# A list scheduler's planning figures replaced by trace durations, and the MLP's squares taken from Pool to Scalar

## The chip, the core and the metric

One core of a Trainium2 chip runs the whole program in one launch. The time is the device time of one execution in microseconds (us). The kernel before took 1974.14 us, the median of three runs (1968.65 to 1974.84). The engines are TensorE (PE in the profile, with its weight loads as PEld), Vector (DVE), Scalar (ACT), Pool (POOL) and Sync (SP), which only issues DMAs.

## What is computed

Two blocks on 512 tokens of width 1024, in float32. The first has two layers, each with a mixer (chunked mLSTM, a Fourier mix and a gated convolution) and an MLP, on the tokens and, in layer 0, on 256 context tokens too. The second is one layer of sparse, windowed, pooled and memory attention. The MLP is the part whose squares change:

```python
def sq_relu_mlp(h, w1, w2):
    return jnp.square(jax.nn.relu(h @ w1)) @ w2

x = x + mx[5] * rmsnorm(sq_relu_mlp(hx, w_mlp1[l], w_mlp2[l]), g_post_mlp[l])
```

## The kernel before

Activations lie transposed, 128 features by tokens. Each large product is done in three passes of a reduced format: an operand x is split into hi (x rounded) and lo (x - hi), and hi*hi, hi*lo and lo*hi are summed in PSUM. `split` makes such a pair with a Scalar copy and a Vector subtraction; `weight` loads a weight block into a `wr` buffer and splits it into `wh` and `wl`. Tiles named `pd`, `pm` and `pa` are PSUM; `slot`, `tmp`, `ftmp` and `small` are SBUF buffers.

The MLP's hidden width of 4096 is worked in eight quarters of four blocks. A block's first product is evacuated by `first` or, for the pairs done by a Strassen scheme in `strassen`, by `fast`'s `tail`: a relu on Scalar, then `square_parts`, which must leave hi and lo of the square for the second product. In the first quarter (`plain`), Vector and Pool also build the Strassen combinations of the inputs (`combos`). Before the MLP of a layer come its mixer, whose mLSTM runs chunk by chunk (`scores`, `values`, `outputs`, `turned`), and the product with w_out (`Wo`, in `layer`).

Nothing is issued as it is written. Every operation is recorded with its dependencies, and `Recorder.schedule` walks a simulated clock: at each moment it gives every free engine the ready operation of the lowest priority number for which buffers are free. `Recorder.cost` says how many nanoseconds an operation takes in that plan, and constants in `schedule` say how much later a dependent operation may start on the same or another engine. The resulting order is then written out by `issue`, each engine working strictly in its own order and waiting by semaphores. So a figure in `cost` changes no instruction; it changes where instructions stand. All recorded operations carry the line of `issue` (L395), so the profile is read by tile names.

Of the kernel before, what the change touches and what calls it, by code (L numbers as in the profile page):

```python
# [13 lines left out]
F32 = mybir.dt.float32  # L14
# [3 lines left out]
AF = mybir.ActivationFunctionType  # L18
ALU = mybir.AluOpType
# [110 lines left out]


class Op:
    __slots__ = ("eng", "fn", "method", "a", "k", "deps", "out", "n", "prio", "bufs", "start", "end", "cost", "dma")


class Recorder:
# [75 lines left out]
    def cost(self, op, out):  # L212
        if out is None:
            return 1300
        if op.dma:
            x = out if isinstance(out, View) else (op.k["in_"] if "in_" in op.k else op.a[1])
            return math.prod(x.shape) * 4 / 330
        n = max(out.idx.size, max((v.idx.size for v in op.a if isinstance(v, View)), default=0))
        if op.eng == "pe":
            if op.method == "transpose":  # L220
                return 110
            lhs = op.a[1]
            n = out.idx.size
            if lhs.dtype == F32R:
                return n / 2.4 + 2 if n >= 256 else 107
            if lhs.dtype == BF:
                return max(n / 2.4, 61)
            c = max(4 * n / 2.4, 217)
            return c / 4 + 26 if lhs.shape[1] <= 32 else c / 2 if lhs.shape[1] <= 64 else c
        ins = [v for v in list(op.a[1:]) + [op.k.get("in_"), op.k.get("in0")] if isinstance(v, View)]  # L230
        psum = any(v.buf.kind in PSUM_KINDS for v in ins)
        if op.eng == "act":
            ap = sum(isinstance(op.k.get(x), View) for x in ("bias", "scale"))
            return (55 if psum else 97) + 0.833 * n + 93 * ap + (93 if "accum_out" in op.k else 0)
        if op.eng == "vec":
            if op.method == "reciprocal":
                return 70 + 8 * n
            if op.method in ("tensor_copy", "tensor_scalar", "memset") and not psum:
                return 70 + 0.55 * n + (120 if op.method == "tensor_scalar" else 0)
            return (135 if op.method == "scalar_tensor_tensor" else 70) + 1.042 * n  # L240
        if op.method == "tensor_tensor":
            return 150 + 2.1 * n
        if op.method == "tensor_scalar":
            return 200 + 3.6 * n
        return 100 + 0.85 * n

    def schedule(self):

        ops = self.ops
# [22 lines left out]
        free = {k: [(0.0, i) for i in range(n or 0)] for k, (n, _) in self.kinds.items()}  # L272
        engs = {"pe": 0.0, "act": 0.0, "vec": 0.0, "pool": 0.0, "sp": 0.0}
# [5 lines left out]
        def push(i, t):  # L279
            heapq.heappush(waiting[ops[i].eng], (t, i))  # L280
# [2 lines left out]
                push(i, 0.0)  # L283
        done = 0
        now = 0.0
        SEM, SLACK, SAME = 120.0, 300.0, {"pe": 0.0, "act": 120.0, "vec": 130.0, "pool": 60.0, "sp": 0.0}
        releases = []

        def place(o):

            new = [b for b in o.bufs if b.place is None]
            got = []
            for b in new:
                n, spare = self.kinds[b.kind]
# [12 lines left out]
                got.append(b)  # L307
            for b in new:
                b.place = heapq.heappop(free[b.kind])[1] if b in got else next(self.names)
            return True  # L310
        while done < N:
            progress = False
            for e in ("sp", "pe", "vec", "act", "pool"):
                while waiting[e] and waiting[e][0][0] <= now:
                    i = heapq.heappop(waiting[e])[1]
                    heapq.heappush(avail[e], (ops[i].prio, i))
                if engs[e] > now or not avail[e]:
                    continue
                skipped, pick = [], None
                if e == "pe" and held is not None:  # L320
                    x = (ops[held].prio, held)
                    if x not in avail[e] or not place(ops[held]):
                        continue
                    avail[e].remove(x)
                    heapq.heapify(avail[e])
                    pick = held
                while avail[e] and pick is None:
                    x = heapq.heappop(avail[e])
                    if place(ops[x[1]]):
                        pick = x[1]  # L330
# [12 lines left out]
                o.start = now  # L343
                if o.dma:
                    issue = {"sp": 60, "act": 60, "pool": 1040}[e]
                    engs[e] = now + issue
                    dma_free[e] = max(dma_free[e], now + issue) + o.cost
                    o.end = dma_free[e] + 1900
                else:
                    engs[e] = o.end = now + o.cost  # L350
                order.append(pick)
                done += 1
                for b in o.bufs:
                    b.left -= 1
                    b.end = max(b.end, o.end)
                    if b.left == 0 and self.kinds[b.kind][0] is not None:
                        heapq.heappush(free[b.kind], (b.end + SEM, b.place))
                        heapq.heappush(releases, b.end + SEM)
                for j in succ[pick]:
                    same = ops[j].eng == e and not o.dma  # L360
                    wait = SAME[e] if same else SEM + (SLACK if ops[j].eng == "pe" else 0)
                    ready_at[j] = max(ready_at[j], o.end + wait)
                    need[j] -= 1
                    if need[j] == 0:
                        push(j, ready_at[j])
            if progress:
                continue
            ts = [t for t in engs.values() if t > now] + [w[0][0] for w in waiting.values() if w and w[0][0] > now]
            while releases and releases[0] <= now:
                heapq.heappop(releases)  # L370
# [27 lines left out]
def tile_net(tc: tile.TileContext, A, out):  # L398
    rec = Recorder(tc.nc, tc, KINDS)
    act, vec, pool, pe, sp = [rec.engine(e) for e in ("act", "vec", "pool", "pe", "sp")]  # L400

    def kind(k):
        return lambda shape=(P, 512), dt=F32: rec.buf(k, shape, dt)
    slot, tmp, ftmp, small, const, rst, pd, pm, pa = [kind(k) for k in ("slot", "tmp", "ftmp", "small", "const", "rs", "pd", "pm", "pa")]

    def A_(out_, in_, f, bias=0.0, scale=1.0):
        return act.activation(out_, in_, f, bias=bias, scale=scale)
# [24 lines left out]
    for l in range(2):  # L432
        t = const([P, NPV], F32)
# [957 lines left out]
    def layer(l, hs, nxt, steps, back, mid, ends, early=None, norm_mem=None, fill=None):  # L1391
# [52 lines left out]

        def second(q, b, g, o):
            w, sl, n = g
# [695 lines left out]
```

## Time and profile before

| | |
|---|---|
| median of 3 runs | 1974.14 us |
| profiled execution | 1975.36 us, span 1973.6 us |
| TensorE matmul busy | 1890.9 us (96%) |
| Vector busy | 1354.0 us (69%) |
| Scalar busy | 908.9 us (46%) |
| Pool busy | 425.8 us (22%) |
| mean granted TensorE clock | 0.980 |

The span runs from the first to the last instruction. A matmul's end is modelled, and matmuls overlap, so the start of one to the start of the next is what it costs in a row. The granted clock is a share of full speed, 2.4 GHz; 0.50 is the lower level, 1.2 GHz. "idle before" names the engine and tile that ended a wait.

### The profile page before, as it was taken

How to read it: one execution, taken by the hardware profiler on the slowest of the kernel's cores; microseconds unless marked ns; L12 is line 12 of the kernel's file. 1: busy time of each engine (PE TensorE's matmuls, PEld its weight loads, DVE VectorE, ACT ScalarE, POOL GpSimd, SP SyncE). 2: the span in 40 equal slices, each digit the busy share in tenths (PEclk: the TensorE clock that was granted, in tenths of full speed). 3: DMA queues.
4: the chain of work that ended last, by engine and by line, in shares of the span. 5: the costliest groups of instructions: out<-in, count | busy, mean ns of one | idle time of the engine just before them, and what ended most of it. 6: DMA issues, size and time to landing. Idle time of an engine off the chain costs nothing.

```text
span 1973.6 us, 32415 instructions
## 1 busy us (share of the span) xinstructions
PE 1890.9 (96%) x12772; PEld 1641.0 (83%) x12772; DVE 1354.0 (69%) x2370; ACT 908.9 (46%) x1786; POOL 425.8 (22%) x438
## 2 busy tenths in 40 slices
PE   5999998998999999999989999889999999999999
PEld 3978886787888999999978888778989889888777
DVE  6499768368356556665677968577787778657686
ACT  4532256564323322332573345655334347556554
POOL 1110042215112211221301023233232221111321
PEclk8999999898999999999999999899999999999999
DMA  8233235243233112211361123352323244311121
GB/s 312 90 110 108 96 109 177 68 150 107 96 118 126 65 56 75 76 65 54 108 216 68 54 86 140 107 171 81 112 86 116 98 137 162 109 54 44 46 84 65
DMA packets 82714, 207.47 MB, mean 105 GB/s; under 512 B 8961, under 2 KB 36865, under 8 KB 82562
## 3 DMA queue, kind: packets, MB, share of 16 engines
q1 hardware_dynamic: 66114, 188.86, 28.0%
q10 hardware_dynamic: 16448, 16.54, 2.5%
q8 instruction: 100, 1.64, 0.3%
q14 instruction: 52, 0.43, 0.1%
HBM read 189.12 MB, written 16.25 MB: 104 GB/s over the span
## 4 chain that ended last, share of the span: by engine, by line
PE 80%; DVE 11%; ACT 3%; DMA 2%; issue 2%; POOL 1%; SPq 0%; DVEq 0%; POOLq 0%; ACTq 0%
PE pd L395 57%; PE pm L395 21%; DVE slot L395 7%; PE pa L395 3%; DVE tmp L395 2%; ACT slot L395 1%; DVE wl L395 1%; DMA wr<-in_w_ada 1%; DVE small L395 1%; ACT tmp L395 1%; DMA wr<-in_w_in 1%; ACT small L395 1%; DMA slot<-in_w_ada 1%; ACT wh L395 0%; DVE ftmp L395 0%
## 5 line engine op out<-in xcount | busy, mean ns | idle before, releaser
L395 PE MATMUL pd<-slot,wh 128*128 128x256 f32 (+2 forms) x4384 | 1092.2, 340 | 14.5 <-DVE slot L395 5.5
L395 PEld LDWEIGHTS pd<-slot,wh 128*128 128x128 f32 (+1 forms) x4384 | 744.7, 189 | 122.0 <-issue 17.5
L395 PE MATMUL pd<-slot,wl 128*128 128x256 f32 (+1 forms) x2136 | 720.9, 339 | 4.9 <-DVE wl L395 4.7
L395 PEld LDWEIGHTS pd<-slot,wl 128*128 128x128 f32 x2136 | 406.8, 191 | 52.1 <-DVE wl L395 6.8
L395 ACT ACTIVATE wh<-wr 128x1024 fp32r<-128x1024 f32 (+2 forms) x202 | 204.9, 1015 | 387.4 <-PE pd L395 356.3
L395 DVE TENSOR_TENSOR wl<-wr,wh 128x1024 fp32r<-128x1024 f32 (+2 forms) x199 | 244.7, 1230 | 128.5 <-ACT wh L395 126.3
L395 PE MATMUL pm<-slot,slot 128*128 128x256 f32 (+3 forms) x1674 | 238.0, 291 | 6.9 <-ACT slot L395 4.0
L395 PEld LDWEIGHTS pm<-slot,slot 128*128 128x128 f32 x1674 | 213.2, 191 | 19.7 <-issue 6.4
L395 DVE TENSOR_TENSOR slot<-pd,slot 128x512 f32<-128x512 f32 (+1 forms) x208 | 119.5, 574 | 122.3 <-PE pd L395 120.4
L395 PE MATMUL pd<-slot,slot 128*128 128x256 f32 (+1 forms) x1048 | 143.0, 285 | 2.4 <-ACT ftmp L395 1.6
L395 PEld LDWEIGHTS pd<-slot,slot 128*128 128x128 f32 x1048 | 130.1, 189 | 8.4 <-issue 3.5
L395 ACT ACTIVATE tmp<-tmp 128x512 f32<-128x512 f32 (+3 forms) x122 | 62.2, 545 | 123.1 <-DVE tmp L395 122.1
L395 DVE TENSOR_TENSOR slot<-ftmp,slot 128x512 fp32r<-128x512 f32 (+2 forms) x116 | 90.9, 786 | 36.5 <-POOL ftmp L395 35.0
L395 DVE SCALAR_TENSOR_TENSOR slot<-slot,const,slot 128x512 f32<-128x512 f32 (+2 forms) x184 | 113.5, 664 | 0.8
L395 POOL TENSOR_TENSOR ftmp<-tmp 128x512 f32<-128x512 f32 x54 | 58.8, 1110 | 214.1 <-ACT tmp L395 214.0
L395 POOL TENSOR_TENSOR ftmp<-ftmp 128x256 f32<-128x256 f32 (+1 forms) x72 | 62.4, 867 | 186.5 <-ACT ftmp L395 154.8
L395 POOL TENSOR_TENSOR wr<-wr 128x512 f32<-128x512 f32 x27 | 39.3, 1456 | 286.4 <-DVE wl L395 247.2
L395 DVE TENSOR_TENSOR slot<-wr,slot 128x512 fp32r<-128x512 f32 (+1 forms) x85 | 86.0, 1018 | 20.8 <-ACT slot L395 20.8
L395 PE MATMUL pm<-slot,wh 128*128 128x256 f32 x544 | 98.4, 281 | 0.0
L395 ACT ACTIVATE slot<-wr 128x512 fp32r<-128x512 f32 (+1 forms) x85 | 72.1, 854 | 44.1 <-POOL wr L395 22.6
L395 ACT ACTIVATE slot<-tmp 128x512 fp32r<-128x512 f32 (+1 forms) x122 | 73.5, 627 | 31.5 <-DVE tmp L395 18.8
L395 PEld LDWEIGHTS pm<-slot,wh 128*128 128x128 f32 x544 | 84.2, 188 | 2.8 <-issue 1.6
(202 smaller groups left out, 2355.3 us busy)
## 6 DMA issues: line engine op xcount, KB each, us to landing
wr<-in_w_mlp SPq DMA_DIRECT2D x128, 512.0 KB, 3.4
wr<-in_w_ada SPq DMA_DIRECT2D x80, 512.0 KB, 3.8
wr<-in_w_in SPq DMA_DIRECT2D x66, 512.0 KB, 3.3
dram<-slot ACTq DMA_DIRECT2D x52, 256.0 KB, 3.3
tmp<-dram SPq DMA_DIRECT2D x40, 256.0 KB, 3.6
slot<-in_w_ada SPq DMA_DIRECT2D x16, 512.0 KB, 9.3
wr<-in_w_out SPq DMA_DIRECT2D x16, 512.0 KB, 4.1
wr<-in_w_out SPq DMA_DIRECT2D x8, 384.0 KB, 2.9
```

The lines of the kernel that those rows point to most:

```text
L395: o.fn(*[conv(x) for x in o.a], **{k: conv(x) for k, x in o.k.items()})
```

## The change

There are two edits. The planner's figures are rewritten: `cost` gets new formulas by engine and shape, and `schedule` gets new waits between engines, a charge of 170 ns where TensorE goes from one array shape to another, and a longer Vector operation where it and a Pool operation both read two tiles from SBUF. And `square_parts` no longer lets Pool multiply the tile with itself: Scalar squares in place, and `split` copies the result to hi on Scalar and subtracts on Vector.

```diff
             lhs = op.a[1]
+            op.mode = tuple(32 if x <= 32 else 64 if x <= 64 else 128 for x in (k, lhs.idx.size if op.method == "transpose" else lhs.shape[1]))
             if lhs.dtype == F32R:
-                return n / 2.4 + 2 if n >= 256 else 107
+                return n * 0.4453 + 4 if n >= 256 else 112
...
         if op.eng == "act":
-            return (55 if psum else 97) + 0.833 * n + 93 * ap + (93 if "accum_out" in op.k else 0)
+            return (150 + 0.86 * n if psum else 190 + 0.847 * n) + 97 * ap + (195 if op.k.get("accum_out") is not None else 0)
         if op.eng == "vec":
...
-            return (135 if op.method == "scalar_tensor_tensor" else 70) + 1.042 * n
+            return (200 if op.method == "scalar_tensor_tensor" else 140) + 1.06 * n
         if op.method == "tensor_tensor":
-            return 150 + 2.1 * n
+            return 200 + 2.1 * n
...
-        SEM, SLACK, SAME = 120.0, 300.0, {"pe": 0.0, "act": 120.0, "vec": 130.0, "pool": 60.0, "sp": 0.0}
+        SAME = {"pe": 0.0, "act": 35.0, "vec": 35.0, "pool": 70.0, "sp": 0.0}
+        SEM, TO = {"pe": 205.0}, {"pe": 420.0, "pool": 80.0}
+        SWITCH, mode = 170.0, None
+        reads = {"vec": 0.0, "pool": 0.0}
...
+                    if e == "pe":
+                        if mode != o.mode:
+                            engs[e] = o.end = o.end + SWITCH
+                        mode = o.mode
+                    elif e in reads and o.shared:
+                        if e == "vec" and reads["pool"] > now:
+                            engs[e] = o.end = o.end + 0.6 * min(reads["pool"] - now, o.cost)
+                        reads[e] = o.end
...
-                    wait = SAME[e] if same else SEM + (SLACK if ops[j].eng == "pe" else 0)
+                    wait = SAME[e] if same else max(SEM.get(e, 40.0), TO.get(ops[j].eng, 0.0))
...
         def square_parts(t, ah, al):
-            A_(ah, t, AF.Square)
-            t2 = ftmp(list(t.shape))
-            pool.tensor_tensor(t2, t, t, op=ALU.mult)
-            vec.tensor_tensor(al, t2, ah.bitcast(F32), op=ALU.subtract)
+            A_(t, t, AF.Square)
+            split(ah, al, t)
```

Where the instructions stand is seen in the order that each engine is given. Scalar, in the first quarter of layer 0's MLP, before: each tile (`ftmp`, from `pd`) has a relu and a square into a `slot`; between them stand the modulations (`tmp` with two `const`) of the context tokens.

```order
L395 ACTIVATE ftmp_676_4449<-pd_620_4129 128x256
L395 ACTIVATE tmp_671_4417<-tmp_671_4417,const_57_258,const_469_3118 128x256
L395 ACTIVATE slot_680_4465<-ftmp_676_4449 128x256
L395 ACTIVATE slot_608_4044<-tmp_671_4417 128x512
L395 ACTIVATE ftmp_682_4479<-pd_622_4136 128x256
```

The same place after the change:

```order
L411 ACTIVATE ftmp_675_4447<-pd_621_4127 128x256
L411 ACTIVATE ftmp_677_4454<-pd_627_4169 128x256
L411 ACTIVATE ftmp_675_4447<-ftmp_675_4447 128x256
L411 ACTIVATE ftmp_677_4454<-ftmp_677_4454 128x256
L411 ACTIVATE slot_681_4473<-ftmp_675_4447 128x256
L411 ACTIVATE slot_682_4480<-ftmp_677_4454 128x256
```

Two tiles now go through relu, square and copy side by side, and the second half of the modulation has moved behind them.

Vector, at the end of that quarter, before. A row `slot<-ftmp,slot` of 256 columns is a square's subtraction, the last one here being that of the ninth tile; rows with `tmp` and 512 columns are the Strassen combinations and their splits; `wl` is a weight's lower half.

```order
L395 TENSOR_TENSOR slot_688_4520<-ftmp_706_4661,slot_688_4520 128x256
L395 TENSOR_TENSOR wl_710_4683<-wr_665_4387,wh_709_4668 128x1024
L395 TENSOR_TENSOR slot_610_4054<-tmp_693_4551,slot_608_4044 128x512
L395 TENSOR_TENSOR slot_694_4556<-ftmp_712_4692,slot_694_4556 128x256
L395 TENSOR_TENSOR slot_711_4687<-tmp_705_4650,slot_711_4687 128x512
L395 TENSOR_TENSOR slot_719_4730<-tmp_701_4614,slot_711_4687 128x512
L395 TENSOR_TENSOR wl_721_4741<-wr_668_4403,wh_717_4717 128x1024
L395 TENSOR_TENSOR slot_680_4465<-ftmp_718_4726,slot_680_4465 128x256
```

After the change, with the ninth tile's subtraction in the fourth row:

```order
L411 TENSOR_TENSOR slot_606_4035<-tmp_679_4463,slot_605_4028 128x512
L411 TENSOR_TENSOR slot_699_4652<-tmp_689_4531,slot_699_4652 128x512
L411 TENSOR_TENSOR wl_703_4687<-wr_664_4382,wh_700_4660 128x1024
L411 TENSOR_TENSOR slot_681_4473<-ftmp_701_4674,slot_681_4473 128x256
L411 TENSOR_TENSOR slot_707_4718<-tmp_680_4465,slot_699_4652 128x512
L411 TENSOR_TENSOR wl_709_4727<-wr_667_4402,wh_705_4708 128x1024
L411 TENSOR_TENSOR slot_682_4480<-ftmp_704_4694,slot_682_4480 128x256
L411 TENSOR_TENSOR slot_707_4718<-tmp_692_4571,slot_707_4718 128x512
L411 TENSOR_TENSOR tmp_712_4759<-slot_619_4123,tmp_695_4610 128x512
```

A weight half, combinations and splits that stood ahead of the ninth tile's subtraction now stand behind it.

TensorE, at the end of the mLSTM of layer 1, before: `pm` with 129 columns are values, the last ones in the first row; `pd` with 512 columns is w_out's product; `pm<-const` are transposes. The rows between the first and the last are all there is between the two.

```order
L395 MATMUL pm_1765_12182<-slot_1652_11663,slot_1611_11443 128x129 x2
L395 MATMUL pd_1753_12134<-slot_1699_11870,wh_1746_12110 128x512 x2
L395 MATMUL pd_1753_12134<-slot_1699_11870,wl_1751_12126 128x512
L395 MATMUL pd_1767_12195<-slot_1694_11852,wh_1760_12156 128x512 x2
L395 MATMUL pd_1767_12195<-slot_1694_11852,wl_1762_12169 128x512
L395 MATMUL pd_1767_12195<-slot_1694_11852,wh_1760_12156 128x512
L395 MATMUL pd_1767_12195<-slot_1697_11863,wh_1760_12156 128x512
L395 MATMUL pd_1767_12195<-slot_1694_11852,wl_1762_12169 128x512
L395 MATMUL pd_1767_12195<-slot_1697_11863,wh_1760_12156 128x512 x2
L395 MATMUL pd_1767_12195<-slot_1697_11863,wl_1762_12169 128x512
L395 MATMUL pd_1767_12195<-slot_1699_11870,wh_1760_12156 128x512 x2
L395 MATMUL pd_1767_12195<-slot_1699_11870,wl_1762_12169 128x512
```

After the change:

```order
L411 MATMUL pm_1698_12129<-slot_1588_11636,slot_1534_11304 128x129
L411 MATMUL pm_1699_12136<-slot_1478_10820,slot_1679_12016 128x129 x2
L411 MATMUL pm_1701_12143<-slot_1588_11636,slot_1543_11375 128x129 x2
L411 MATMUL pd_1687_12072<-slot_1641_11839,wh_1632_11803 128x512
L411 MATMUL pd_1687_12072<-slot_1641_11839,wl_1635_11818 128x512
L411 MATMUL pm_1702_12160<-const_33_130,slot_1657_11907 128x128
L411 MATMUL pm_1703_12162<-const_33_130,ftmp_1629_11796 128x128 x2
```

Fifteen of w_out's matmuls stood behind the last values; two do now, and the others stand ahead of them.

## Rows read from the trace of the kernel before

**Rows 1.** The page, part 1: busy us, share of the span and instructions by engine.

```profile
PE 1890.9 (96%) x12772; PEld 1641.0 (83%) x12772; DVE 1354.0 (69%) x2370; ACT 908.9 (46%) x1786; POOL 425.8 (22%) x438
```

**Rows 2.** Span and mean granted clock of the core.

```profile
core 0: 1973.6 us, clock 0.980
```

**Rows 3.** Windows: length, PE, PEld, DVE, ACT, POOL busy (count), clock, DMA share, GB/s.

```profile
450.00:500.00 50.00, 45.59 (x305) 39.08 (x305) 38.63 (x46) 24.58 (x53) 27.17 (x22) 0.90 0.21 74
700.00:750.00 50.00, 50.00 (x345) 46.32 (x344) 28.48 (x40) 13.91 (x21) 9.59 (x8) 1.00 0.13 43
1300.00:1350.00 50.00, 42.34 (x298) 37.18 (x299) 40.91 (x48) 26.38 (x55) 27.09 (x22) 0.97 0.33 119
```

**Rows 4.** Windows, same columns: two stretches of low clock, and one ahead.

```profile
487.60:494.40 6.80, 6.08 (x18) 4.85 (x19) 2.96 (x10) 2.47 (x6) 1.57 (x2) 0.50 0.23 78
1225.00:1235.00 10.00, 8.19 (x48) 6.70 (x47) 10.00 (x39) 7.83 (x26) 0.00 (x0) 1.00 0.34 125
1235.10:1245.40 10.30, 5.79 (x14) 3.14 (x15) 4.29 (x9) 8.17 (x24) 2.24 (x2) 0.50 0.00 0
```

**Rows 5.** In order of time, steady MLP: start, us, engine, line, operation, out<-in.

```profile
697.28 1.14 ACT L395 ACTIVATE slot<-tmp 128x512 fp32r<-128x512 f32 x2
...
699.85 0.68 DVE L395 TENSOR_TENSOR slot<-ftmp,slot 128x512 fp32r<-128x512 f32 x1
```

**Rows 6.** Groups by form, 450 to 500: count, busy us, mean ns, idle before.

```profile
L395 POOL TENSOR_TENSOR ftmp<-ftmp 128x256 f32<-128x256 f32 x12 | 11.7, 973 | 8.5 <-ACT ftmp L395 8.3
...
L395 DVE TENSOR_TENSOR slot<-tmp,slot 128x512 fp32r<-128x512 f32 x12 | 13.0, 1093 | 0.0
L395 DVE TENSOR_TENSOR slot<-ftmp,slot 128x256 fp32r<-128x256 f32 x12 | 9.1, 759 | 0.5 <-ACT ftmp L395 0.5
...
L395 ACT ACTIVATE slot<-ftmp 128x256 fp32r<-128x256 f32 x12 | 4.9, 412 | 0.2
```

**Rows 7.** Groups by form, 1300 to 1350.

```profile
L395 POOL TENSOR_TENSOR ftmp<-ftmp 128x256 f32<-128x256 f32 x12 | 11.0, 920 | 26.4 <-issue 21.5 <-DVE slot L395 2.4 <-PE pm L395 1.8
...
L395 DVE TENSOR_TENSOR slot<-tmp,slot 128x512 fp32r<-128x512 f32 x12 | 10.5, 898 | 0.0
L395 DVE TENSOR_TENSOR slot<-ftmp,slot 128x256 fp32r<-128x256 f32 x12 | 10.1, 844 | 1.3 <-POOL ftmp L395 1.3
```

**Rows 8.** TensorE's waits, 450 to 500: us in total, times, longest.

```profile
PE pd L395 <- DVE slot L395: 2.6, 2, 2.2
PE pd L395 <- ACT ftmp L395: 1.6, 1, 1.6
```

**Rows 9.** TensorE's longest waits, 1300 to 1350.

```profile
PE pd L395 <- DVE wl L395: 4.2, 2, 3.4
```

**Rows 10.** In order of time, 480 to 490, Vector and Pool.

```profile
483.15 1.75 POOL L395 TENSOR_TENSOR tmp<-tmp,slot 128x512 f32<-128x512 f32 x1
...
483.66 1.52 DVE L395 TENSOR_TENSOR slot<-ftmp,slot 128x256 fp32r<-128x256 f32 x1
485.10 1.28 DVE L395 TENSOR_TENSOR slot<-tmp,slot 128x512 fp32r<-128x512 f32 x2
...
487.86 0.41 DVE L395 TENSOR_TENSOR slot<-ftmp,slot 128x256 fp32r<-128x256 f32 x1
```

**Rows 11.** In order of time, TensorE at five places, with idle time before.

```profile
145.58 0.66 PE L395 MATMUL pm<-const,slot 128*128 128x128 f32 x4 [2.81 <-DVE slot L395]
...
425.45 0.80 PE L395 MATMUL pm<-tmp,const 128*128 128x256 f32 x1 [4.42 <-DVE tmp L395]
...
475.93 3.11 PE L395 MATMUL pd<-slot,slot 128*128 128x256 f32 x24 [1.63 <-ACT ftmp L395]
...
1223.70 0.48 PE L395 MATMUL pd<-slot,wh 128*128 128x512 f32 x1
...
1236.12 0.86 PE L395 MATMUL pm<-const,slot 128*128 128x128 f32 x2 [2.93 <-ACT slot L395]
```

**Rows 12.** In order of time, Scalar, the split of w_out's weight.

```profile
1222.02 1.04 ACT L395 ACTIVATE wh<-wr 128x1024 fp32r<-128x1024 f32 x1
```

More of the change, by code (lines that the diff above doesn't have):

```diff
@@ L132 @@
 class Op:
-    __slots__ = ("eng", "fn", "method", "a", "k", "deps", "out", "n", "prio", "bufs", "start", "end", "cost", "dma")
+    __slots__ = ("eng", "fn", "method", "a", "k", "deps", "out", "n", "prio", "bufs", "start", "end", "cost", "dma", "mode", "shared")
 class Recorder:
@@ L219, in cost @@
         if op.eng == "pe":
+            lhs = op.a[1]
+            k = lhs.p1 - lhs.p0
+            op.mode = tuple(32 if x <= 32 else 64 if x <= 64 else 128 for x in (k, lhs.idx.size if op.method == "transpose" else lhs.shape[1]))
             if op.method == "transpose":
                 return 110
-            lhs = op.a[1]
             n = out.idx.size
             if lhs.dtype == F32R:
-                return n / 2.4 + 2 if n >= 256 else 107
+                return n * 0.4453 + 4 if n >= 256 else 112
@@ L226, in cost @@
             if lhs.dtype == BF:
-                return max(n / 2.4, 61)
-            c = max(4 * n / 2.4, 217)
-            return c / 4 + 26 if lhs.shape[1] <= 32 else c / 2 if lhs.shape[1] <= 64 else c
+                return max(n / 2.4 + 2.5, 61)
+            c = max(4 * n / 2.4 + 5, 219)
+            return c / 4 + 2 if op.mode == (128, 32) else c / 2 if op.mode == (128, 64) else c
         ins = [v for v in list(op.a[1:]) + [op.k.get("in_"), op.k.get("in0")] if isinstance(v, View)]
         psum = any(v.buf.kind in PSUM_KINDS for v in ins)
+        op.shared = len(ins) > 1 and not psum
@@ L232, in cost @@
         if op.eng == "act":
-            ap = sum(isinstance(op.k.get(x), View) for x in ("bias", "scale"))
-            return (55 if psum else 97) + 0.833 * n + 93 * ap + (93 if "accum_out" in op.k else 0)
+            ap = any(isinstance(op.k.get(x), View) for x in ("bias", "scale"))
+            return (150 + 0.86 * n if psum else 190 + 0.847 * n) + 97 * ap + (195 if op.k.get("accum_out") is not None else 0)
         if op.eng == "vec":
             if op.method == "reciprocal":
-                return 70 + 8 * n
+                return 137 + 8 * n
@@ L238, in cost @@
             if op.method in ("tensor_copy", "tensor_scalar", "memset") and not psum:
-                return 70 + 0.55 * n + (120 if op.method == "tensor_scalar" else 0)
-            return (135 if op.method == "scalar_tensor_tensor" else 70) + 1.042 * n
+                return (200 if op.method == "tensor_scalar" else 150) + 0.65 * n
+            return (200 if op.method == "scalar_tensor_tensor" else 140) + 1.06 * n
         if op.method == "tensor_tensor":
-            return 150 + 2.1 * n
+            return 200 + 2.1 * n
@@ L243, in cost @@
         if op.method == "tensor_scalar":
-            return 200 + 3.6 * n
-        return 100 + 0.85 * n
+            return 350 + 2.8 * n
+        return 110 + 0.85 * n
     def schedule(self):
@@ L356, in schedule @@
                     if b.left == 0 and self.kinds[b.kind][0] is not None:
-                        heapq.heappush(free[b.kind], (b.end + SEM, b.place))
-                        heapq.heappush(releases, b.end + SEM)
+                        heapq.heappush(free[b.kind], (b.end + 120.0, b.place))
+                        heapq.heappush(releases, b.end + 120.0)
                 for j in succ[pick]:
                     same = ops[j].eng == e and not o.dma
-                    wait = SAME[e] if same else SEM + (SLACK if ops[j].eng == "pe" else 0)
+                    wait = SAME[e] if same else max(SEM.get(e, 40.0), TO.get(ops[j].eng, 0.0))
                     ready_at[j] = max(ready_at[j], o.end + wait)
```

## The prediction

> **What bounds the kernel now.** I read the page first, then the clock, then windows of 50 us, then what TensorE waits for in the windows that are not full, then single stretches instruction by instruction. TensorE is busy 1890.9 us of 1973.6 [rows 1], and the change touches no matmul. So the time can move only where TensorE is not fed: 82.7 us without a matmul, and the stretches in which its clock is at the lower of its two levels (the mean granted clock is 0.980 [rows 2], which is some 40 us at full speed). The windows show where. From 700 to 750 us, in the middle of an MLP, TensorE is busy 50.00 of 50.00 at clock 1.00, and nothing that another engine saves there counts. From 450 to 500 and from 1300 to 1350, at the start of the two MLPs, it is busy 45.59 and 42.34, the clock is 0.90 and 0.97, and Vector and Pool are at their busiest [rows 3]. The kernel is a full engine with some forty small holes; a new order closes some and opens others.
> A wait costs more than its length. With the one that ends at 488.3 the granted clock falls to 0.50 (1.2 GHz) for 6.80 us, with the one before 1236.12 for 10.30 us [rows 4]. A matmul takes twice as long there, so up to 3.4 and 5.1 us go on top.
>
> **The squares.** 106 tiles (54 of 512 columns, 52 of 256) lose Pool's product and gain a Scalar copy. Vector's subtraction stays and reads the squared tile instead of Pool's.
> Most of this is hidden. In the steady MLP of layer 0 the last two tiles of a Strassen product show the tightest case: Scalar squares both from 697.28 in 1.14 us, Vector ends the last subtraction at 700.53 [rows 5]. Without Pool, Scalar copies both right behind, until about 699.5 (another pair, 1.05 to 1.14 us), and the last subtraction (0.68) ends at about 700.2. Equal or 0.3 us earlier, and TensorE does not idle there. Price 0; bounds per round: nothing gained, since the engine is full, or 0.5 us lost; over seven rounds 0 to +3.5 us. Scalar's extra work, 54 x 0.6 + 52 x 0.41 = 54 us [rows 5, 6], lies where Scalar is busy 14 to 26 of 50 us [rows 3].
>
> It isn't hidden in the first quarter of either MLP, where Vector is the bound: TensorE waits 2.6 us for Vector's slot tiles and 1.6 us for a square's Scalar chain in the first stretch, 4.2 us for Vector's weight halves in the second [rows 8, 9]. Pool slows Vector there. The subtraction of 256 columns takes 0.41 us at 487.86, with Pool idle, and 1.52 us at 483.66, while Pool is in a tensor_tensor from 483.15 to 484.90 [rows 10]. Over the first stretch its mean is 0.759 us, and that of the 512 column splits 1.093 [rows 6] against 0.68 alone [rows 5]: 12 x 0.35 + 12 x 0.41 = 9.1 us of Vector's time that Pool costs. Pool's squares are 11.7 of its 27.2 us there [rows 3, 6], 43%, so 3.9 us go with them. In the second stretch the same sum is 12 x 0.434 + 12 x 0.218 = 7.8 us, the squares are 11.0 of 27.1 us [rows 3, 7], and 3.2 us go. Scalar, which takes over, gets 12 x 0.41 = 4.9 us in each stretch, beside 25 and 26 us.
> The new order helps in the first stretch as well. The subtraction for which TensorE waits until 488.3 stood behind most of the Strassen combinations on Vector; several of them now stand behind it, some 6 us of Vector's work.
> I take away 2.4 us of waits for Vector in the first stretch (all but 0.2 of them) and 3.1 in the second, together 5.5, and 3.1 of the low clock that comes with them (3.4 us in the first; in the second a mean of 0.97 over 50 us, 1.5). Bounds: nothing, if Scalar's longer chain takes Vector's place; and all of it, 4.2 + 4.2 + 4.9 = 13.3 us. **Term: -8.6 us.**
>
> **The planner's numbers.** They shift instructions everywhere, yet on TensorE the neighbourhood of most waits stays: the same matmuls stand around the waiting one, moved by a few microseconds. I price a shift with 0.12 us for a matmul of 256 columns (24 of them in the 2.94 us from 475.93 [rows 11]) and 0.23 for one of 512. Three waits get more cover: the one of 2.81 us before 145.58, the one of 4.42 before 425.45 [rows 11], and the first one's repeat in layer 1, before 1092.3. TensorE's work ahead of them grows by 1.0, 2.6 and 0.9 us, Vector's by -0.5, 1.2 and 0.0: together 3.8 us gained. In the start-up eleven matmuls fewer stand ahead of a wait near 51, up to 1.3 us lost, and 0.5 at the one before it; I take half, 0.9. At the end of the mLSTM of layer 1, fifteen matmuls of w_out (512 columns) stood between the last values and the transposes that wait; now two do. 13 x 0.23 = 3.0 us of cover is gone, and the wait of 2.93 us before 1236.12 [rows 11] can become 5.9. It need not: Vector is busy 10.00 of 10.00 us from 1225 to 1235 [rows 4], and where it is behind anyway, values that come later cost nothing. Bounds 0 and 3.0, I take 1.5. Sum of what I can place: -3.8 + 0.9 + 1.5 = -1.4. New waits can't be seen in the old trace, and a new order makes some; I set them at +1.4, so this term is **0**. Its bounds: -16.5 (the three waits wholly gone, 10.1 us, and with each a low clock of at most the 3.4 us priced above, less the 3.8 counted), and +7, rival C.
> I credit the plan with no more because its new figures are not the time for which an engine is held. A 512 column tensor_tensor is now planned as 140 + 1.06 x 512 = 683 ns, which is what one shows, but two in a row from 485.10 take 1.28 us [rows 10]: the second starts after 0.60, and 603 ns is what the old formula gave.
> The Trainium skill (Perfetto Trace Analysis, Optimizing Scalar/DVE Operations) speaks against the change in the same way: a profiled duration contains a tail that overlaps the next instruction. By that rule the planner's term is 0 or worse; taking durations as occupancy it would be -3.8.
> Loads: as many DMAs are issued, and SP's list has as many rows; I leave them at 0, bounds within those of this term.
>
> **Sum.** The profiled execution took 1975.36 us (the span of 1973.6 and 1.8 around it), 1.2 over the median of 1974.14. 1975.4 - 8.6 + 0 = 1966.8; counted from the median, 1965.5. I say 1966.
>
> **Rivals.**
> A. The order pays as well: the three waits with more cover go (6.3 us beyond the 3.8), and half of the low clock with them (5.1). 1966 - 11.4 = 1955. For it: the cover grows at all three. Against: only 3.8 of the 10.1 us are in the order.
> B. The squares give nothing: TensorE waits for relu, square and copy on Scalar where it waited for Vector, or for the combinations that were moved back. 1974. For it: one wait in the first stretch (1.63 us before 475.93 [rows 11]) already names Scalar. Against: Scalar has half its time free there.
> C. Slower, at the end of the mLSTM of layer 1. The w_out matmuls are spent early: 3.0 us. They also stand 2.9 us earlier in TensorE's work, while their split weight was ready at 1223.06 for a use at 1223.70 [rows 11, 12], so up to 2.3 us of a new wait. A longer hole can lengthen the 10.30 us of low clock there [rows 4]; by a third, that is 1.7 lost. 7.0 us; with the squares giving nothing, 1982. It decides from the point where Vector is no longer behind TensorE at 1225, and wins over the forecast where the squares give less than 7.
>
> **Chances.** The forecast (the squares pay, the plan is even) 0.45, its own range 1958 to 1973; A 0.15; B 0.20; C 0.20. A measurement of this kernel can tell 0.3%, 5.9 us, from no change, so faster is under 1968.2 and slower over 1980.1. Of the forecast 0.33 lies under 1968.2 and 0.12 above it; A is faster; B is 0.19 within and 0.01 above; C is slower. Faster 0.48, same 0.31, slower 0.21. The range reaches past A's time and to C's: 1950 to 1982.
>
> **What would show it.** Right: in both first quarters Pool is busy about 16 us instead of 27, the 256 column subtraction's mean is nearer 0.41 than 0.76, TensorE's waits for Vector are under 3 us in each, and the clock is 1.00 in at least one; from 500 to 950 TensorE stays full. Wrong: the subtraction's mean is unchanged (then Pool's other work slowed it), the waits for Scalar pass 3 us in either stretch, the hole at the end of the layer 1 mLSTM passes 4 us before its first transposes, or the steady MLP gets holes of more than 5 us in sum.

## The result: slower by 0.8%

The changed kernel takes 1989.59 us, the median of four runs (1985.91 to 1991.44), beside 1973.14 for the kernel before in the same comparison. The ratio is 1.0077, with a 95% interval of 1.006 to 1.0094. 1966 was predicted, within 1950 to 1982; rival C, the slower one, had the right sign and the right mixer stage, the layer 1 mLSTM, but named its end, and the loss comes ahead of it.

The page's first part for the changed kernel, which answers to [rows 1]:

```profile
PE 1891.8 (95%) x12772; PEld 1645.0 (83%) x12772; DVE 1317.6 (66%) x2370; ACT 953.3 (48%) x1892; POOL 322.5 (16%) x332
```

and its span and granted clock, to [rows 2]:

```profile
core 0: 1988.8 us, clock 0.977
```

TensorE's work is the same, its idle time has gone from 82.7 to 97.0 us, and Pool lost 103 us, the 106 squares. Windows of the changed kernel, with the columns of [rows 3]:

```profile
450.00:500.00 50.00, 47.68 (x344) 41.72 (x345) 35.41 (x56) 31.04 (x71) 16.36 (x10) 0.93 0.36 127
...
1200.00:1250.00 50.00, 34.93 (x240) 30.17 (x238) 35.39 (x111) 25.99 (x78) 13.19 (x10) 0.87 0.21 76
...
1300.00:1350.00 50.00, 41.50 (x334) 35.62 (x333) 36.95 (x52) 26.36 (x59) 13.41 (x8) 0.97 0.46 156
...
500.00:950.00 450.00, 450.00 (x3228) 414.25 (x3228) 242.71 (x378) 169.15 (x283) 36.66 (x28) 1.00 0.24 82
```

From 1200 to 1250 TensorE was busy 42.63 us before; now it is 34.93. To see where time goes I laid the traces side by side at equal counts of TensorE's matmuls. The table has the microseconds that each kernel takes longer (+) or shorter (-) than the kernel before for the same number of them. The stretches are in the time of before; the columns after the first belong to experiments told below. They come from one profiled execution each, and where a boundary falls beside a wait, about 1 us can pass from one row to the next.

| stretch of before | changed | e1 | e2 | e6 | e9 | e11 |
|---|---|---|---|---|---|---|
| 0 to 289, start, layer 0 mixer | +1.9 | -1.2 | +0.2 | +2.1 | 0.0 | -2.6 |
| 289 to 460, its mLSTM, w_out | +3.6 | -0.3 | +3.0 | +2.3 | -4.9 | -3.2 |
| 460 to 512, MLP's first quarter | -9.0 | -3.6 | -3.4 | -8.8 | -7.6 | -9.0 |
| 512 to 976, rest of the MLP | +1.0 | +0.3 | +0.2 | +1.1 | -0.6 | -0.6 |
| 976 to 1203, layer 1 mixer | -0.3 | -0.9 | -5.1 | -2.5 | -6.4 | -5.9 |
| 1203 to 1264, its mLSTM | +16.6 | +0.3 | +16.7 | +5.2 | +1.7 | +1.0 |
| 1264 to 1358, w_out, first quarter | -0.8 | +2.8 | +0.6 | -0.1 | +1.2 | -6.1 |
| 1358 to the end | +2.2 | -0.1 | +4.0 | +3.4 | 0.0 | 0.0 |
| sum | +15.2 | -2.7 | +16.2 | +2.7 | -16.6 | -26.4 |

So one stretch of 60 us carries the loss. TensorE's waits in the changed kernel from 1200 to 1255 (us in total, times, longest):

```profile
PE pm L411 <- ACT slot L411: 7.2, 2, 6.8
PE pd L411 <- POOL slot L411: 4.9, 2, 4.3
PE pd L411 <- DVE small L411: 2.9, 1, 2.9
```

The 6.80 us are those of the transposes at the mLSTM's end. They look like the 2.93 of before [rows 11] more than doubled, but a second wait stood there before, four transposes later:

```profile
1240.53 0.86 PE L395 MATMUL pm<-const,slot 128*128 128x128 f32 x2 [2.27 <-ACT slot L395]
```

With the short ones between, the transposes' waits there were 6.4 us in sum and are 9.0. At equal counts some 14 of the 16.6 us are lost before TensorE comes to this end, by 1224 in the time of before: in the waits of 4.9 and 2.9 us, and in the low clock behind each, where the granted clock had been 1.00 from 1203 to 1235. In the changed kernel:

```profile
1205.50:1213.00 7.50, 6.64 (x32) 5.23 (x33) 4.71 (x5) 4.21 (x7) 6.97 (x5) 0.56 0.69 258
1225.90:1230.00 4.10, 4.10 (x25) 3.95 (x26) 2.84 (x9) 1.39 (x5) 0.00 (x0) 0.61 0.02 4
```

The 4.9 us are new and come first. They are a wait for Pool's product into Rt, a table that `scores` needs. Scalar and Pool around it in the changed kernel:

```profile
1202.24 1.06 ACT L411 ACTIVATE wh<-wr 128x1024 fp32r<-128x1024 f32 x1 [13.14 <-DMA wr<-in_w_out]
1203.21 1.21 ACT L411 ACTIVATE slot<-tmp 128x512 fp32r<-128x512 f32 x2
...
1203.90 3.76 POOL L411 TENSOR_TENSOR slot<-slot,const 8x512 fp32r<-8x512 f32 x3 [6.49 <-ACT slot L411]
```

and in the kernel before, the same copy and product:

```profile
1195.18 0.63 ACT L395 ACTIVATE slot<-tmp 128x512 fp32r<-128x512 f32 x1 [8.25 <-DMA tmp<-in_ohr]
...
1195.89 1.03 POOL L395 TENSOR_TENSOR slot<-slot,const 8x512 fp32r<-8x512 f32 x1 [2.13 <-ACT slot L395]
```

The first copy runs 8.0 us later than before. Scalar stood still for 13.14 us in front of a weight split whose load had not landed, with Rt's copies next in its list, but that is not what made them late: the table that is copied had not landed either. Its two loads, the rows of SP that issue them and their size and median time to landing, in the changed kernel:

```profile
1197.02 0.33 SPq L411 DMA_DIRECT2D wr<-in_w_out  x1
1197.44 1.01 SPq L411 DMA_DIRECT2D tmp<-in_ohr  x2
...
tmp<-in_ohr SPq DMA_DIRECT2D x2, 256.0 KB, 5.5
```

and before:

```profile
1192.62 1.68 SPq L395 DMA_DIRECT2D tmp<-in_ohr  x2
...
tmp<-in_ohr SPq DMA_DIRECT2D x2, 256.0 KB, 2.5
```

The first load was issued 4.8 us later and took 3 us longer to land (5.4 us at the least), at 1202.8, 0.4 us before its copy began; so the split in front cost at most these 0.4 us. Why the load took longer is not shown; a load of w_out is issued just ahead of it. It was issued late because of its buffer. It is loaded into a `tmp` buffer, and the planner hands those out strictly in the order of the program; ahead of it stand the ten `tmp` of the mLSTM's recurrence, and ahead of these the norm of the convolution's output (`conv_norm`). That norm's squares ran on Scalar at 1173.92 and 1175.05 before and at 1176.99 and 1177.82 now. So the recurrence moved, and with it the release of its buffers. TensorE in the kernel before, with the recurrence (`pm<-tmp,slot`) between matmuls of the gate product (`pd<-slot,wh`):

```profile
1183.70 1.05 PE L395 MATMUL pm<-tmp,slot 128*128 128x129 f32 x8
1184.51 0.71 PE L395 MATMUL pd<-slot,wh 128*128 128x512 f32 x2
1185.06 1.05 PE L395 MATMUL pm<-tmp,slot 128*128 128x129 f32 x8
```

and in the changed kernel:

```profile
1185.35 0.40 PE L411 MATMUL pd<-slot,wl 128*128 128x512 f32 x1
1185.59 1.05 PE L411 MATMUL pd<-slot,slot 128*128 128x128 f32 x8
1186.57 1.07 PE L411 MATMUL pa<-wr,const 128*32 128x256 f32 x16
1187.57 1.61 PE L411 MATMUL pm<-tmp,slot 128*128 128x129 f32 x12
```

The whole product is spent before the recurrence starts, 3.9 us later than before; only the small `pa` products are left to fill it, and they run out at 1201.2.

### The profile page after: what moved, and what is told of

The parts are those of the page before. It is cut to its first block, busy times and chain, and to the rows that moved or that the text cites. A ratio compares the mean times of both kernels' runs of the same rounds, so it can differ in the third digit from the quotient of the medians.

```text
span 1988.8 us, 32360 instructions
## 1 busy us (share of the span) xinstructions
PE 1891.8 (95%) x12772; PEld 1645.0 (83%) x12772; DVE 1317.6 (66%) x2370; ACT 953.3 (48%) x1892; POOL 322.5 (16%) x332
## 4 chain that ended last, share of the span: by engine, by line
PE 85%; DVE 7%; ACT 3%; DMA 3%; issue 1%; POOL 1%; SPq 0%; ACTq 0%; DVEq 0%; POOLq 0%
PE pd L411 60%; PE pm L411 22%; DVE slot L411 4%; PE pa L411 3%; DVE tmp L411 1%; DMA wr<-in_w_ada 1%; ACT slot L411 1%; DVE wl L411 1%; ACT tmp L411 1%; DVE small L411 1%; POOL slot L411 1%; DMA wr<-in_w_out 0%; ACT small L411 0%; ACT wh L411 0%; DMA tmp<-in_ohr 0%
## 5 line engine op out<-in xcount | busy, mean ns | idle before, releaser
L411 PE MATMUL pd<-slot,wh 128*128 128x256 f32 (+2 forms) x4384 | 1088.3, 340 | 16.6 <-ACT slot L411 7.9
L411 PE MATMUL pd<-slot,slot 128*128 128x256 f32 (+1 forms) x1048 | 147.6, 289 | 17.4 <-POOL slot L411 6.7
L411 ACT ACTIVATE tmp<-tmp 128x512 f32<-128x512 f32 (+4 forms) x176 | 90.7, 567 | 128.4 <-DVE tmp L411 127.5
L411 POOL TENSOR_TENSOR wr<-wr 128x512 f32<-128x512 f32 x27 | 35.2, 1305 | 624.2 <-DVE wl L411 406.8
L411 DVE SCALAR_TENSOR_TENSOR slot<-slot,const,slot 128x512 f32<-128x512 f32 (+1 forms) x184 | 112.7, 665 | 0.8
L411 DVE TENSOR_TENSOR slot<-tmp,slot 128x512 fp32r<-128x512 f32 x114 | 80.7, 731 | 30.8 <-ACT slot L411 30.4
L411 ACT ACTIVATE slot<-slot 128x512 f32<-128x512 f32 (+9 forms) x114 | 67.0, 610 | 32.7 <-DVE slot L411 28.8
L411 PE MATMUL pm<-const,slot 128*128 128x128 f32 (+2 forms) x380 | 61.1, 282 | 20.2 <-ACT slot L411 12.7
```

Source lines behind the costliest of these rows:

```text
L411: o.fn(*[conv(x) for x in o.a], **{k: conv(x) for k, x in o.k.items()})
```

## The experiments

Ratios are to the kernel before, timed alongside, with 95% intervals.

**The two edits apart.** e1 is the kernel before with the new `square_parts`; e2 is the changed kernel with the old one.

> Only the squares change; the planner keeps the figures of before. Theory 1 (the squares pay, the planner's figures lose it all and more): the stretch 450 to 500 gives back what it gave in the changed kernel, 8.8 us, and the one from 1300 to 1350 some more, now that TensorE does not come to it out of a hole: 1974 - 9 to 12 = 1962 to 1965 us, ratio 0.994 to 0.996. Theory 2 (the squares pay only where the new order has moved the combinations behind the ninth tile): TensorE still waits about 2 us for the ninth tile's chain and the clock still falls behind it, 1970 to 1974. Theory 3 (Scalar's longer chain is what hurts, the planner is innocent): 1980 or more.

> Only the planner's figures change; the squares are those of before, with Pool. Theory 1: the holes at the ends of both mLSTM stages (8 us in layer 0, 14 to 17 in layer 1), 2.7 for the weight half at 991 and 2 in the start-up stand as they are, and the first quarters lose what the squares gave: 1974 + 24 = 1998, 1994 to 2002. Theory 2 (the squares pay only with the new order): as much or more, up to 2002. Theory 3: the planner is innocent and this kernel is at 1966 to 1976.

e1: 1972.99 us, 0.9997 (0.9986 to 1.0009). e2: 1990.13, 1.0088 (1.007 to 1.0107). e2 lies under the ranges of its theories 1 and 2 and far over that of 3: the planner's figures make the whole loss, and the squares alone give nothing in the old order. For e1 theory 2 is nearest. Its Scalar in the first quarter of layer 0, up to the ninth tile's copy, and TensorE behind it:

```profile
483.89 0.63 ACT L395 ACTIVATE slot<-tmp 128x512 fp32r<-128x512 f32 x1 [3.99 <-POOL tmp L395]
484.42 0.36 ACT L395 ACTIVATE ftmp<-pm 128x256 f32<-128x256 f32 x1
484.82 0.42 ACT L395 ACTIVATE ftmp<-ftmp 128x256 f32<-128x256 f32 x1
485.27 0.42 ACT L395 ACTIVATE slot<-ftmp 128x256 fp32r<-128x256 f32 x1
...
485.74 1.04 PE L395 MATMUL pd<-slot,wh 128*128 128x256 f32 x2 [3.39 <-ACT slot L395]
```

The wait for Vector [rows 8] is gone, and one for Scalar has taken its place. The tile's relu, square and copy stand behind the split of a Strassen combination that Pool has not finished. This is rival B's mechanism.

**Which figures.** e3 takes back the shape charge, e4 the waits between operations, e10 the durations.

```diff
-        SWITCH, mode = 170.0, None                                     # e3
+        SWITCH, mode = 0.0, None
-        SAME = {"pe": 0.0, "act": 35.0, "vec": 35.0, "pool": 70.0, "sp": 0.0}   # e4
-        SEM, TO = {"pe": 205.0}, {"pe": 420.0, "pool": 80.0}
+        SAME = {"pe": 0.0, "act": 120.0, "vec": 130.0, "pool": 60.0, "sp": 0.0}
+        SEM, TO = {e: 120.0 for e in engs}, {"pe": 420.0}
```

> The changed kernel with one planning figure taken back: TensorE is no longer charged 170 ns where it goes from one array shape to another (0 instead). If this charge is what spends the fillers early (in the mLSTM, where nearly every second group has another shape, it makes TensorE late in the plan and everything beside it early), the holes of 4.9, 2.9 and 6.8 us at the layer 1 mLSTM are smaller by more than half and the time is 1972 to 1980. If the waits between engines or the longer durations do it, the same holes stand and it is 1986 to 1994.

> The changed kernel with the waits between operations taken back to those of before (120 ns between engines, 420 to TensorE, 120 and 130 on Scalar and Vector behind themselves); durations, shape charge and squares stay new. If the tight waits are the cause (Scalar and Vector chains that look shorter than they are, so that the plan leaves no slack), the holes at the layer 1 mLSTM shrink by more than half: 1972 to 1980. If the durations or the shape charge are, 1986 to 1994.

> The changed kernel with the durations taken back to those of before; the new waits, the shape charge, the charge for shared reads and the squares stay. With e4_oldwaits and e1_squares it tells durations from waits. Theory 1 (the shorter waits put each chain's next step too close, and the durations only soften it): slower than the changed kernel, 1995 to 2010. Theory 2 (the longer durations make the plan of Scalar crowded, which delays the norm): near before, 1970 to 1980.

e3: 1992.94, 1.0112 (1.0089 to 1.0134): taking the shape charge back gives nothing. e4: 1978.32, 1.0024 (1.0011 to 1.0036), in its first range, though the layer 1 mLSTM still loses 8.8 of the 16.6 us. e10: 1982.93, 1.0048 (1.003 to 1.0067), between its two theories. The percentages add: 0.24 with the new durations, 0.48 with the new waits (both charges stay in either), 0.77 with all, and -0.03 (e1) with none. No single group of figures is at fault. That the shares add this well can be chance, since an order changes in jumps.

**The place.** e6 raises the norm of the convolution's output in layer 1, e8 loads Rt's table into another kind of buffer, and e7 is e4 with the norm raised in both layers.

```diff
-        conv_norm()
+        with rec.urgent(2000 * l):              # e6; e7: (500, 2000)[l]
+            conv_norm()
...
-            t = tmp([P, 4, P])                  # e8
+            t = ftmp([P, 4, P])
             ld(t, A["ohr"][:, d])
```

> The changed kernel with one block of layer 1 moved: the norm of the convolution's output gets a higher priority in the plan. In the changed kernel's trace this norm runs 3 us late on Scalar, its tmp buffers come ahead of those of the mLSTM's recurrence, so the recurrence's 40 matmuls start 4 us late, behind all of the gate product that stood between them before; then Rt is late and TensorE waits 4.9 us for Pool's Rt product. Theory 1 (this late norm is the root of the hole at 1200 and of what follows to 1255): most of the 16.6 us lost there come back, 1975 to 1980. Theory 2 (the root is Scalar's order, where Rt's copies stand behind a w_out split that waits for its load; the norm is only early or late): the wait for Rt stays at 4 us or more and the time is 1986 to 1992.

> The changed kernel with one buffer changed: the table from which Rt is made is loaded into an ftmp buffer, so it does not queue behind the ten tmp buffers of the recurrence. Theory 1 (the late norm is the root): only the wait for Rt in layer 1 goes, 4.3 + 0.6 us and what clock comes with it, 1982 to 1986; the recurrence still starts late. Theory 2 (Rt's place behind the load and the split is the root): all that follows goes too, 12 to 16 us, 1973 to 1978.

> The kernel with the new durations and squares and the old waits between operations (1978.3 us) with the norm of the convolution's output raised in both layers. It lost 4.2 and 8.8 us against before on the way through layer 1's mixer and mLSTM and 4.6 in layer 0's. Theory 1 (the late norm is the root in both layers): 10 or more of these come back and the kernel is faster than before, 1962 to 1969. Theory 2 (the root lies elsewhere): 1975 to 1980.

e6: 1976.84, 1.0017 (1.0007 to 1.0026). One moved norm takes 12.8 us off the changed kernel's median, 11.4 of them in its table row of +16.6. Its waits from 1195 to 1260:

```profile
PE pm L411 <- ACT slot L411: 6.0, 1, 6.0
PE pd L411 <- ACT wh L411: 1.8, 1, 1.8
PE pd L411 <- DVE small L411: 1.2, 1, 1.2
```

No wait for Pool's Rt is left: theory 1. What is left of the row's 5.2 us comes ahead of the mLSTM's end, in the waits of 1.8 and 1.2 us and a granted clock of 0.71 from 1220 to 1225.9. The 6.0 us at the end again hold both waits of before: all waits of these transposes are 7.2 us beside 6.4. e8: 1985.59, 1.0057 (1.004 to 1.0074), 4 us off, which is what theory 1 allows for Rt's own wait (its profiled execution took 1980.09, 5.5 us under its median, so its stretches are not used). e7: 1973.79, 1.0002 (0.999 to 1.0015), between its theories: the way to 1203 gave 4 us back and the mLSTM 1.7 (8.8 to 7.1), but the 4 us and more of layer 0's mLSTM stayed, though its norm's squares ran some 10 us earlier than in e4. There the late norm is not the root. In the changed kernel the longest new wait there is 5.3 us, for a `pd` of `scores`; why the plan makes it was not tried. Nor is it shown which of the new figures put layer 1's norm late.

**Only the good stretches.** e5 plans the mixers and block 2 with all figures of before. e9 is meant to beat both kernels: new durations, charges and squares, the old waits of e4, and the figures of before from the query convolutions to the end of each mixer and in block 2.

```diff
         op.cost = self.cost(op, outs[0] if outs else None)
+        op.old = self.old
+        if op.old:
+            op.cost = self.cost_before(op, outs[0] if outs else None)
...
+        rec.old = True                               # e9; in e5 ahead of mixers()
         qt = [slot([P, 2, CW]) for _ in range(2)]
...
             parts_of_y((0, 1, 2, 3))
+        rec.old = False
         return ys
```

> The changed kernel, but the operations of the two mixers (everything ahead of w_out in a layer) and of block 2 are planned with the figures of before; start-up, w_out and both MLPs keep the new ones, and the squares are the new ones. Theory 1 (the new figures lose their time in the mixers' order alone, and the gain at the first quarter of layer 0 comes from the new order there): 1974, less 9 at the first quarter of layer 0, 0 to 3 back at the one of layer 1: 1964 to 1969. Theory 2 (the new figures lose wherever they plan; the mixers only show it first): the holes come back at w_out or in the MLP's start, 1976 or more.

> A version meant to beat both: the new durations and squares with the old waits; and from the query convolutions of each mixer to its end (the norm, the mLSTM) and in block 2, all figures of before. Theory 1 (the new figures lose only there): what each stretch gave in the earlier runs adds up: about -2 by 180 us, 0 over the layer 0 mLSTM, -8 at the first quarter of layer 0, -5 at 991 and -2.8 near 1138 (both as with the old waits), 0 over the layer 1 mLSTM, -1 after it: -17 against before, 1955 to 1961. Theory 2 (the stretches do not add up; a list plan shifts everything behind an edit): 1964 to 1974.

e5: 1969.82, 0.998 (0.997 to 0.9989). e9: 1957.76, 0.9917 (0.9899 to 0.9936). Both are within 1 us of theory 1: the stretches add up, and the new figures are good ahead of the mLSTM and in the MLP.

**Pool's other work.** In e9 the first quarter of layer 1 still has a wait of 3.77 us for a weight half (`wl`) on Vector. What Vector and Pool do ahead of it is plain in the changed kernel, where the same wait is 3.9 us and ends with the half in the fifth row; Vector's rows and Pool's:

```profile
1335.57 2.32 DVE L411 TENSOR_TENSOR wl<-wr,wh 128x1024 fp32r<-128x1024 f32 x1
1337.81 1.77 DVE L411 TENSOR_TENSOR tmp<-tmp,slot 128x512 f32<-128x512 f32 x1
1339.50 2.96 DVE L411 TENSOR_TENSOR slot<-ftmp,slot 128x256 fp32r<-128x256 f32 x2
1342.38 1.75 DVE L411 TENSOR_TENSOR tmp<-tmp,slot 128x512 f32<-128x512 f32 x1
...
1344.72 1.21 DVE L411 TENSOR_TENSOR wl<-wr,wh 128x1024 fp32r<-128x1024 f32 x1
...
1335.12 1.68 POOL L411 TENSOR_TENSOR tmp<-slot,tmp 128x512 f32<-128x512 f32 x1 [0.63 <-DVE tmp L411]
1336.77 2.26 POOL L411 TENSOR_TENSOR tmp<-slot,slot 128x512 f32<-128x512 f32 x1
1339.00 4.58 POOL L411 TENSOR_TENSOR tmp<-tmp,slot 128x512 f32<-128x512 f32 x3
```

Pool's first operation here ends at 1336.80, and Vector's first half, begun at 1335.57, ends 1.09 us after that; alone it takes 1.21. Pool's next one begins at 1336.77 and ends 1.14 us after Vector's half does. They take turns. The Trainium skill (SBUF — State Buffer, SBUF: two separate sides) says so: Vector with two SBUF inputs and a Pool operation that reads SBUF share one port pair, and whoever starts first has it for the whole instruction. Here the trace agrees. The half that TensorE waits for is not slowed itself, 1.21 us with Pool done; it is late because Vector's list ahead of it is. From 1335.57 to 1344.72 Vector takes 9.15 us, and by the steps from start to start of undisturbed rows (1.14 us for a half, 0.60 for 512 columns, 0.33 for 256) I estimate 3.7. e11 is e9 with Pool's half of the Strassen combinations on Vector, e12 is e9 with the squares on Pool again, e13 has both of these edits, and e14 is the kernel before with the new squares and e11's edit.

```diff
-                t1, t3 = diff(vec, b12, b11), diff(pool, b22, b12)
+                t1, t3 = diff(vec, b12, b11), diff(vec, b22, b12)
                 t2 = rest(vec, b22, t1)
-                t4 = rest(pool, b21, t2)
+                t4 = rest(vec, b21, t2)
```

> The version of e9_mlstm_old with Pool's half of the Strassen combinations of the inputs given to Vector, so that Pool has nothing to do at the start of either MLP. Theory 1 (in the first quarter of layer 1 Pool's combinations, not its squares, slow Vector: 2.32 us for a weight half that takes 1.21 alone): the 256 column subtraction's mean falls to 0.41 to 0.45 in both first quarters, Vector takes ten more products of some 0.6 to 0.7 us a layer and loses its slow ones, and the time is 0 to 5 us below e9_mlstm_old. Theory 2 (Vector's own work is the bound there): it is 3 to 10 us above it.

> The version of e9_mlstm_old with the squares of before, on Pool. Theory 1 (the squares pay about 6 us, but only in an order that keeps the chains of Scalar clear): 5 to 8 us above e9_mlstm_old, lost in the first quarters. Theory 2 (the new order alone gives the gain at the first quarter, the squares nothing): within 2 us of it.

> The version of e11_combos_vec with the squares back on Pool: Pool has the squares, Vector all of the combinations. Theory 1 (each Pool product slows Vector alike; the squares, 11 of Pool's 27 us in a first quarter, slow it too): the 256 column subtraction's mean is between 0.45 and 0.8 and the time 2 to 6 us above e11_combos_vec, 1952 to 1956. Theory 2 (only the combinations matter; a square's product ends before Vector needs the port for long): within 2 us of e11_combos_vec.

> The kernel before, its planner untouched, with the new squares and with Pool's half of the combinations on Vector. Theory 1 (the squares gave nothing alone because Pool's combinations went on slowing Vector, and made Scalar wait 4.0 us for a tmp of Pool ahead of the ninth tile): the wait of 3.4 us at 482 and those for wl near 1320 go, with the low clock behind them, 1960 to 1966. Theory 2 (the old order itself keeps the ninth tile's chain behind the combinations): 1968 to 1973.

| | combinations shared with Pool | combinations on Vector |
|---|---|---|
| squares on Pool | e12: 1960.38, 0.9939 (0.9923 to 0.9954) | e13: 1952.94, 0.9892 (0.9875 to 0.9909) |
| squares on Scalar | e9: 1957.76, 0.9917 (0.9899 to 0.9936) | e11: 1949.53, 0.9883 (0.9864 to 0.9901) |
| the same, planner of before | e1: 1972.99, 0.9997 (0.9986 to 1.0009) | e14: 1956.66, 0.9911 (0.9892 to 0.9931) |

The combinations are worth 0.34 to 0.47% with the new planner and 0.86 with the old; the squares 0.1 to 0.2%, with intervals that overlap. e12, 2.6 us above e9, lies between its theories. e11 and e14 do better than their theory 1. e11 has the lowest median, 1.2% under the kernel before; its interval and e13's overlap. Its windows at the two first quarters answer to [rows 3]:

```profile
450.00:500.00 50.00, 50.00 (x361) 45.78 (x360) 30.52 (x55) 29.56 (x64) 0.00 (x0) 1.00 0.23 78
1280.00:1330.00 50.00, 48.99 (x354) 43.23 (x350) 36.41 (x63) 33.03 (x72) 2.60 (x2) 0.97 0.34 118
```

and its subtractions of 256 columns in both, by form, to [rows 6, 7] (`issue` is at L453 in these kernels):

```profile
L453 DVE TENSOR_TENSOR slot<-ftmp,slot 128x256 fp32r<-128x256 f32 x12 | 5.0, 421 | 1.0 <-ACT slot L453 1.0
...
L453 DVE TENSOR_TENSOR slot<-ftmp,slot 128x256 fp32r<-128x256 f32 x12 | 4.8, 419 | 0.9 <-ACT slot L453 0.8
```

e9's windows, for comparison:

```profile
450.00:500.00 50.00, 49.11 (x355) 44.79 (x354) 34.64 (x46) 29.39 (x67) 13.13 (x9) 1.00 0.25 84
1280.00:1330.00 50.00, 42.06 (x296) 36.68 (x295) 35.39 (x48) 27.79 (x64) 16.50 (x10) 0.90 0.34 118
```

and its subtraction in the first of them:

```profile
L453 DVE TENSOR_TENSOR slot<-ftmp,slot 128x256 fp32r<-128x256 f32 x12 | 8.1, 681 | 0.5 <-ACT slot L453 0.5
```

In e11 Vector has all of the combinations and yet is less busy from 450 to 500, 30.52 us against 34.64: it no longer waits inside its instructions. Over the whole run it is busy 1304.1 us beside 1312.6 in e9, with twenty operations more. In e13, where Pool has only squares, the mean lies between, 460 and 555 ns, as its theory 1 had it.

## Why the prediction was wrong

**The planner's term is the step that failed.** It was set at 0, with new waits at +1.4 and a bound of +7. Alone (e2) it is 0.88%, some 17 us. The new waits were taken as small because the old trace can't show them; one of them, with the late work and the low clock behind it, is most of the 16.6 us. The three places were the wrong ones to look at: I compared what stands ahead of the old waits. What made the new one could in part be read in the order: on TensorE the whole gate product ahead of the recurrence, whose `tmp` buffers the table needs. Scalar's list, with the split ahead of Rt's copies, looks as telling, but cost at most 0.4 us. The rule of the Trainium skill that stood beside this term (Perfetto Trace Analysis, Optimizing Scalar/DVE Operations: a profiled duration has a tail that overlaps the next instruction) had the sign, but e4 and e10 give the durations a third of the loss, and e9 gains with them.

**The old waits.** All three shrank: 2.81 to 1.71 us before 145 and 2.9 to 1.8 before 1092, near what was priced, and 4.42 to 3.61 before 425, less than priced; together 3.0 of the 3.8.

**The end of the layer 1 mLSTM.** Fifteen w_out matmuls became two, and I took 1.5 of the 3.0 us of cover. The wait of 6.80 us passes the 5.9 that I set as the most, but only because the prediction looked at the first of two waits: the changed order does the statistics of the last two chunks one behind the other, and 2.93 and 2.27 us became one. The transposes' waits grew by 2.6 us in the changed kernel and by 0.8 in e6, both within the bounds. So this term held. Rival C priced the whole loss here, with a new wait for the split weight beside it; that wait came in e6 alone, 1.8 of the 2.3 us allowed. Its sign came true for another reason, 20 to 40 us earlier, at the recurrence's start.

**The squares.** What they free on Vector was right: over the first stretch the subtraction's mean went from 759 to 548 ns and the split's from 1093 to 886, 12 x 0.21 + 12 x 0.21 = 5.0 us where 3.9 were worked out (4.7 in e1, with the squares alone). These are by form the changed kernel's rows for both stretches:

```profile
L411 DVE TENSOR_TENSOR slot<-tmp,slot 128x512 fp32r<-128x512 f32 x12 | 10.5, 886 | 3.9 <-ACT slot L411 3.9
...
L411 DVE TENSOR_TENSOR slot<-ftmp,slot 128x256 fp32r<-128x256 f32 x12 | 6.5, 548 | 0.9 <-ACT slot L411 0.8
...
L411 DVE TENSOR_TENSOR slot<-ftmp,slot 128x256 fp32r<-128x256 f32 x9 | 5.6, 660 | 0.0
```

What that is worth was mis-sized: 8.6 us were set, and alone (e1) the squares give 0.03%, 0.6 us. Layer 0's first quarter gave 9.0 us in the changed kernel, more than the 8.6 for both layers, but that is luck; the order alone gives 3.4 there (e2) and the squares alone 3.6 (e1), and the rest needs both. Layer 1's share never came, since Pool's combinations hold up what stands on Vector ahead of the weight half for which TensorE waits:

```profile
PE pd L411 <- DVE wl L411: 3.9, 1, 3.9
```

That is 4.2 before [rows 9]. Sharing Pool's slowing out by busy time (43%) took all of Vector's operations as alike; only what meets Vector's list ahead of the awaited operation counts. In layer 1 that is the combinations: in e11 and e13, where Pool has none, no wait for `wl` is left from 1280 to 1330. e1 lost what it won elsewhere in layer 1, 2.8 us.

**The signs I named.** Pool is busy 16.36 and 13.41 us, as said. The subtraction's mean is nearer to 0.41 in layer 0 only. Waits for Vector are nil in layer 0 and over 3 us in layer 1. The clock is 0.93 and 0.97, not 1.00, in layer 0 behind 3.1 us of waits for w_ada's loads ahead of the quarter; from 460 to 520 it is 1.00. From 500 to 950 TensorE is full. The hole at the mLSTM's end passed 4 us: this sign of being wrong fired, though most of that hole had stood there before as two.

## What to carry to other kernels

A list scheduler with figures nearer to the traced durations does not give a better order by itself: here one norm planned 3 us late cost more than all that the figures gained elsewhere. Not tried is whether the program's hand-set priorities (`rec.hp += 3000` around the recurrence is one) fit only the old figures; e6 moves just such a priority. Read a new order for what stands in front of what on the engines that are not the bound, and for which buffers are handed out behind which, and not only around the old waits. Take a long idle time in front of a load for a cause only when what stands behind it was ready: here it was 13.14 us long and cost at most 0.4. Compare the sum of the waits of a stage, not the longest one. Where two engines slow each other, take away the whole of one's work in the stretch, or look first which of its pieces meets the operation that is waited for.

## What was not expected of the hardware

Vector and Pool do not slow each other by a share but take turns. A weight half of 1024 columns takes 1.21 us on Vector alone and 2.32 against Pool, a subtraction of 256 columns 0.42 with Pool idle and a mean of 0.68 with 13 to 17 us of Pool's products in 50, and ten products of 512 columns, 0.685 us each on Vector, cost it less than it had lost by waiting for Pool to do them.
